# Joining the high and low token parts in one 512-column product of the gate and up matmuls of a two-layer macaron trunk

## The chip, the cores and the metric

The kernel runs on one core of one Trainium2 chip. The metric is device time in microseconds (us) of one execution. Before the change three runs gave a median of 1028.43 us (1027.76 to 1029.43). Engines are named as the profile does: PE multiplies matrices (PEld is its loading of weights), DVE and ACT work element by element, POOL is used here for small vectors and memsets, SP issues nearly all DMAs.

## The reference

Two layers on 256 tokens of width 1024, all in float32. Each layer is a feed-forward block, an attention mixer, and a second feed-forward block; each has its own modulation (shift, scale, gate) out of the vector `c`.

```python
def swiglu(h, w_gate, w_up, w_down):
    return (jax.nn.silu(h @ w_gate) * (h @ w_up)) @ w_down

for l in range(2):
    mod = silu(c) @ ada_w[l] + ada_b[l]             # nine rows of 1024
    sh1, sc1, g1, sh2, sc2, g2, sh3, sc3, g3 = split(mod, 9)
    h = rmsnorm(x, norm_pre[l, 0]) * (1 + sc1) + sh1
    x = x + 0.5 * g1 * rmsnorm(swiglu(h, ...[l, 0]), norm_post[l, 0])
    h = rmsnorm(x, norm_pre[l, 1]) * (1 + sc2) + sh2
    x = x + g2 * rmsnorm(hybrid_mixer(h, ...), norm_post[l, 1])
    h = rmsnorm(x, norm_pre[l, 2]) * (1 + sc3) + sh3
    x = x + 0.5 * g3 * rmsnorm(swiglu(h, ...[l, 1]), norm_post[l, 2])
```

`hybrid_mixer` projects to heads of 64, runs windowed attention on eight heads and block attention on the other eight, and projects back. The hidden width of a feed-forward block is 2816.

## The kernel before

**Products in three parts.** PE works here on the type float32r, which keeps less than float32. Each operand is therefore split: `hi` is the operand rounded to float32r, `lo` is the rest. A product is the sum of three: high by high, high by low, low by high. For weights, `unit` (from L427) loads 1 MB by DMA into a `raw` buffer (three of them); in four or eight pieces ACT writes `hi` (L437) and DVE writes `lo` = raw - hi (L438). For the tokens, `to_T` (from L586) transposes the normed rows on PE, ACT writes the high part (L594) and DVE the low part (L595). They lie in two tiles, `hTh` and `hTl`, each `[128, half, k-tile, 128 tokens]`, with two halves of 128 tokens and eight k-tiles of the width 1024.

**A feed-forward block** (`ffn`, from L664) has two ways to multiply. The first 512 hidden columns go by token half (`rows_of`): tokens stand still in PE, 512 weight columns move. The other 2304 columns go in nine blocks `j` of 256. There the weights stand still and the 256 tokens move, so the result comes out transposed, ready for the down product. For each `j`, gate and up each have a weight unit (`u_both`); for each of its two groups `t` of 128 hidden columns and each of the eight k-tiles, `mm3t` (L480 to L486) issues three products of 256 columns:

```python
nc.tensor.matmul(ps_, wh, hh, start=start, stop=False)   # L484
nc.tensor.matmul(ps_, wh, hl, start=False, stop=False)   # L485
nc.tensor.matmul(ps_, wl, hh, start=False, stop=stop)    # L486
```

The result of both `t` fills one PSUM bank, one for gate and one for up. `swiglu` then applies Silu on ACT (L640, PSUM to SBUF), multiplies with up on DVE (L641, one operand in PSUM), and `split` makes the high and low part of the result (L634 on ACT, L635 on DVE). `down` takes a unit of `w_down` and issues products of 512 columns with `mm3` (L476 to L478) into four banks of accumulators that are kept over the block. PSUM has eight banks: four accumulators, and two buffers under each of two tags for everything else.

**The background.** While the products run, the modulation rows of later steps are computed: `ada_part` loads 512 KB of `ada_w` (L509), DVE sums it (L501), and `over_partitions` (L516 to L519) splits the sum and reduces it over the partitions on PE. A table (`SEC`) says how much of it each step takes.

**The mixer** takes its columns through `mm3t` too (`cols_of`), and its keys through `keys_of`, which clears a tile `kz` with two memsets on POOL (L740, L741) before the keys are copied in. POOL also works out the inverse norms (`rstd_of`, L572 and L574).

**The order.** `keep_order` (from L77) takes the whole program of some 8,000 instructions, gives each a length with `cost` (from L50), plays it through forward (each engine takes the ready instruction of best priority) and backward (how late may each start), four rounds, keeps the shortest, and fixes that order on every engine. An instruction waits in that order even if a later one of its engine is ready. Which instructions depend on each other is found from the ranges of addresses that they touch; a strided access counts as one range from its first to its last element.

Of the kernel before, what the change touches and what calls it, by code (L numbers as in the profile page):

```python
# [11 lines left out]
F32R = mybir.dt.float32r  # L12
# [3 lines left out]
P = 128  # L16
# [34 lines left out]
def cost(ins, eng, slots):  # L51

    kind = type(ins).__name__
    free = math.prod(c for _, c in list(ins.outs[0].ap)[1:])
    if kind == "InstDMACopy":
        return 4 * free * ins.outs[0].ap[0][1] / 360
    if kind == "InstMatmult":
        if ins.is_transpose:
            return 109
        if "float32r" in str(ins.ins[0].dtype):  # L60
            return max(free, 256) / 2.4 + 2.5
        whole = max(4 * free / 2.4 + 4, 160)
        return whole / 4 if ins.outs[0].ap[0][1] == 32 else whole
    src = getattr(ins.ins[0], "bass_ap", None) if ins.ins else None
    psum = src is not None and slots.get(src.tensor.name, "  ")[2] == "PSUM"
    more = [math.prod(c for _, c in list(x.ap)[1:]) for x in ins.ins[1:] if hasattr(x, "ap")]
    if eng == "Activation":
        return (52 if psum else 94) + free / 1.2 + 93 * (len(more) + len(ins.outs) - 1)
    if eng == "DVE":
        if free <= 8:  # L70
            return 75
        single = kind in ("InstTensorScalarPtr", "InstTensorCopy") and max(more, default=1) == 1 and not psum
        return 69 + free / (1.92 if single else 0.96) + 60 * more.count(1)
    return 264 if kind == "InstTensorScalarPtr" else 464


def keep_order(tc, nc, slots, shifts):  # L77
# [20 lines left out]
    for k, ins in enumerate(L):  # L98
        touch = []
        for w, lst in ((False, ins.ins), (True, ins.outs)):  # L100
            for x in lst:
                b = getattr(x, "bass_ap", None)
                if b is None or type(b.tensor).__name__ != "Tile":
                    continue
                name, row = b.tensor.name, math.prod(list(b.tensor.shape)[1:])
                ap, space = list(x.ap), slots[name][2]
                lo = 0 if space == "PSUM" else b.offset if space == "DRAM" else b.offset % row
                hi = 1 << 30
                if space != "PSUM":
                    hi = lo + 1 + sum(abs(s) * (c - 1) for s, c in (ap if space == "DRAM" else ap[1:]))  # L110
                touch.append((w, name, lo, hi))
        for w, name, lo, hi in touch:
# [183 lines left out]
def trunk(ctx, tc, x, c, rel_bias, ada_w, ada_b, norm_pre, norm_post, w_gate, w_up,  # L296
# [176 lines left out]
    def mm3(ps_, hh, hl, wt, wk, sl, start, stop):  # L473
# [4 lines left out]
        nc.tensor.matmul(ps_, hl, wh, start=False, stop=stop)  # L478

    def mm3t(ps_, kt, wt, sl, start, stop):  # L480

        wh, wl = wt[0][:, kt, sl], wt[1][:, kt, sl]
        hh, hl = hT[0][:, :, kt, :], hT[1][:, :, kt, :]
# [92 lines left out]

    hT = [ctile([P, 2, KT, P], f"hT{n}", F32R) for n in "hl"]

# [7 lines left out]
    def to_T(h, k0, nk, src, turned=False):  # L586
# [3 lines left out]
        for t in range(nk):  # L590
            nc.tensor.transpose(p_[:, t * P:(t + 1) * P], src[:, t * P:(t + 1) * P], ident)
        hi, lo = (hT[n][:, h, k0:k0 + nk, :] for n in range(2))
        v = back(p_[:, :nk * P]) if turned else p_[:, :nk * P].rearrange("p (a b) -> p a b", b=P)
# [50 lines left out]
    def rows_of(h, pair, get):  # L644

        for p_, g in zip(pair, get):
            for q in range(2):
                w = g(q)
                for k in range(4):
                    kt = q * 4 + k  # L650
                    mm3(p_, hT[0][:, h, kt, :], hT[1][:, h, kt, :], w, k, slice(0, 512), kt == 0, kt == 7)

# [7 lines left out]
    def ffn(l, i, first):  # L660
# [21 lines left out]
        for j in range(9):  # L682
            cur[0] = j % 2
            if first and j == SETUP:
                with shift(START_SMALL):
                    setup_table(*small)
            pair = (wps(), wps())
            for p_, (tag, ws) in zip(pair, (("g", w_gate), ("u", w_up))):
                w = u_both(l, f, ws, tag, j)
                for t in range(2):  # L690
                    for k in range(KT):
                        mm3t(p_[:, t * 256:(t + 1) * 256], k, w, slice(t * P, (t + 1) * P), k == 0, k == KT - 1)
            act = split(swiglu(*pair), 512)
            for h in range(2):
# [55 lines left out]
    def mixer(h, l):  # L750
# [10 lines left out]
        for k in range(8):  # L761
            mm3(p_[:, :256], hT[0][:, h, k, :], hT[1][:, h, k, :], w, k, slice(0, 256), k == 0, k == 7)
        b_ = brow(512, 256)
# [99 lines left out]
        for u in range(4):  # L863
            w = u_out(l, u)
            for n in range(2):
                for k in range(2):
                    kt = u * 2 + k
                    mm3(accs[n], hT[0][:, h, kt, :], hT[1][:, h, kt, :], w, k, slice(n * 512, (n + 1) * 512),
                        kt == 0, kt == 7)
# [82 lines left out]
    for q in range(4):  # L952
# [12 lines left out]
        for h in range(2):  # L965
# [82 lines left out]
```

## Time and profile before

| | |
|---|---|
| median of three runs | 1028.43 us (1027.76 to 1029.43) |
| the profiled execution | 1027.23 us, its span 1025.5 us |
| PE busy | 1005.2 us, 98% of the span |
| PEld busy (beside PE) | 893.9 us, 87% |
| DVE busy | 800.5 us, 78% |
| ACT busy | 553.5 us, 54% |
| POOL busy | 42.0 us, 4% |
| DMA | 261.95 MB, 255 GB/s over the span |

The span is the profiled execution from its first to its last instruction. A busy share is a mean over stages of different kinds: six steps follow each other (block, mixer, block, twice), the first mixer at about 225 to 345 us, the second at about 715 to 845 us.

### The profile page before, as it was taken

The numbers are of one execution on the slowest core, as the hardware profiler recorded it, in microseconds if no ns is written. First come the engines' busy times: TensorE is split into PE (matmuls) and PEld (weight loads), VectorE is DVE, ScalarE is ACT, GpSimd is POOL, SyncE is SP. The second block draws the span as 40 slices with busy tenths as digits, with TensorE's granted clock in tenths as the row PEclk, the third lists the DMA queues.
The fourth block names the chain that finished last, engine by engine and source line by source line (L and its number), as shares of the span: only waits on it lengthen the run. The fifth ranks groups of instructions, "written<-read, shape, count | busy, mean of one in ns | idle before, by whom it ended". The sixth has DMA issues, their size and how long they took to land. (4 is left out here: it accounts for less than half of the span.)

```text
span 1025.5 us, 17316 instructions
## 1 busy us (share of the span) xinstructions
PE 1005.2 (98%) x6514; PEld 893.9 (87%) x6514; DVE 800.5 (78%) x1493; ACT 553.5 (54%) x1250; POOL 42.0 (4%) x80
## 2 busy tenths in 40 slices
PE   7999999999999999999999999999999999999997
PEld 3699998978887899999979999998798779999996
DVE  4799888978887898798889888886879788555542
ACT  2456443665677665555465445444477766544431
POOL 1000000020002000000010000000100110000000
PEclk9999999999999999999999999999999999999999
DMA  9999998958994588898839887886589638555511
GB/s 328 365 361 325 313 284 295 343 175 279 311 306 168 207 291 295 285 316 311 290 122 308 298 290 284 303 288 226 168 301 323 209 127 272 193 181 189 184 64 41
DMA packets 171855, 261.95 MB, mean 255 GB/s; under 512 B 6396, under 2 KB 107484, under 8 KB 171772
## 3 DMA queue, kind: packets, MB, share of 16 engines
q1 hardware_dynamic: 171616, 260.78, 75.3%
q8 instruction: 51, 0.84, 0.3%
q14 instruction: 32, 0.26, 0.1%
q10 hardware_dynamic: 156, 0.07, 0.0%
HBM read 259.76 MB, written 1.07 MB: 254 GB/s over the span
## 5 line engine op out<-in xcount | busy, mean ns | idle before, releaser
L438 DVE TENSOR_TENSOR lo_a<-raw_a,hi_a 128x512 fp32r<-128x512 f32 (+1 forms) x540 | 294.1, 593 | 43.9 <-issue 23.4
L437 ACT ACTIVATE hi_a<-raw_a 128x512 fp32r<-128x512 f32 (+1 forms) x540 | 259.9, 547 | 123.3 <-PE w_a L485 25.7
L484 PE MATMUL w_a<-hTh,hi_a 128*128 128x256 f32 x768 | 218.9, 285 | 0.6 <-ACT kz_a L733 0.6
L485 PE MATMUL w_a<-hTl,hi_a 128*128 128x256 f32 x768 | 217.8, 284 | 0.0
L486 PE MATMUL w_a<-hTh,lo_a 128*128 128x256 f32 x768 | 217.3, 283 | 0.0
L484 PEld LDWEIGHTS w_a<-hTh,hi_a 128*128 128x128 f32 x768 | 147.1, 192 | 2.2 <-ACT kz_a L733 0.8
L485 PEld LDWEIGHTS w_a<-hTl,hi_a 128*128 128x128 f32 x768 | 147.1, 192 | 1.2 <-issue 0.3
L486 PEld LDWEIGHTS w_a<-hTh,lo_a 128*128 128x128 f32 x768 | 147.0, 191 | 0.4
L485 PE MATMUL w_b<-hTl,hi_b 128*128 128x256 f32 x512 | 144.8, 283 | 0.0
L484 PE MATMUL w_b<-hTh,hi_b 128*128 128x256 f32 x512 | 144.8, 283 | 0.0
L486 PE MATMUL w_b<-hTh,lo_b 128*128 128x256 f32 x512 | 144.7, 283 | 0.0
L437 ACT ACTIVATE hi_b<-raw_b 128x512 fp32r<-128x512 f32 (+1 forms) x224 | 105.1, 544 | 71.3 <-DMA raw_b<-in_ffn_w_up_dram 16.5
L438 DVE TENSOR_TENSOR lo_b<-raw_b,hi_b 128x512 fp32r<-128x512 f32 (+1 forms) x224 | 119.9, 588 | 22.9 <-issue 17.1
L484 PEld LDWEIGHTS w_b<-hTh,hi_b 128*128 128x128 f32 x512 | 98.1, 192 | 1.0
L485 PEld LDWEIGHTS w_b<-hTl,hi_b 128*128 128x128 f32 x512 | 98.1, 192 | 0.9
L486 PEld LDWEIGHTS w_b<-hTh,lo_b 128*128 128x128 f32 x512 | 98.1, 192 | 0.2
L501 DVE SCALAR_TENSOR_TENSOR acc_a<-araw_a,ccol,acc_a 128x512 f32<-128x512 f32 x110 | 82.2, 747 | 12.5 <-DMA araw_a<-in_ada_w_dram 11.0
L477 PE MATMUL a_b<-lo_a,str_a 128*128 128x512 f32 x156 | 60.8, 392 | 0.0
L476 PE MATMUL a_b<-hi_a,str_a 128*128 128x512 f32 x156 | 60.3, 392 | 0.0
L478 PE MATMUL a_b<-hi_a,str_a 128*128 128x512 f32 x156 | 60.2, 390 | 0.0
L501 DVE SCALAR_TENSOR_TENSOR acc_b<-araw_b,ccol,acc_b 128x512 f32<-128x512 f32 x46 | 34.5, 749 | 6.4 <-DMA araw_b<-in_ada_w_dram 5.5
L478 PE MATMUL w_b<-hi_a,hTl 128*128 128x512 f32 (+1 forms) x96 | 36.5, 380 | 0.0
(245 smaller groups left out, 1723.8 us busy)
## 6 DMA issues: line engine op xcount, KB each, us to landing
araw_a<-in_ada_w_dram SPq DMA_DIRECT2D x84, 512.0 KB
raw_a<-in_ffn_w_down_dram SPq DMA_DIRECT2D x30, 1024.0 KB
raw_a<-in_ffn_w_gate_dram SPq DMA_DIRECT2D x26, 1024.0 KB
raw_a<-in_ffn_w_up_dram SPq DMA_DIRECT2D x26, 1024.0 KB
araw_b<-in_ada_w_dram SPq DMA_DIRECT2D x44, 512.0 KB
raw_a<-in_mix_w_in_dram SPq DMA_DIRECT2D x18, 1024.0 KB
raw_b<-in_ffn_w_gate_dram SPq DMA_DIRECT2D x16, 1024.0 KB
raw_b<-in_ffn_w_up_dram SPq DMA_DIRECT2D x16, 1024.0 KB
```

The costliest lines, as they stand in the source:

```text
L437: nc.scalar.activation(hi[:, sl], raw[:, sl], AF.Copy)
L438: nc.vector.tensor_sub(lo[:, sl], raw[:, sl], hi[:, sl].bitcast(F32))
L476: nc.tensor.matmul(ps_, hh, wh, start=start, stop=False)
L477: nc.tensor.matmul(ps_, hh, wl, start=False, stop=False)
L478: nc.tensor.matmul(ps_, hl, wh, start=False, stop=stop)
L484: nc.tensor.matmul(ps_, wh, hh, start=start, stop=False)
L485: nc.tensor.matmul(ps_, wh, hl, start=False, stop=False)
L486: nc.tensor.matmul(ps_, wl, hh, start=False, stop=stop)
L501: nc.vector.scalar_tensor_tensor(acc[:, :n], raw[:, t, :], ccol[:, k:k + 1], b if t == 0 else acc[:, :n], op0=ALU.mult, op1=ALU.add)
```

## The change

There are four parts.

1. The two token tiles become one, `hTa`, `[128, k-tile, high/low, half, 128]`, so that for one k-tile the 256 high and the 256 low columns lie side by side. A new `mm2t` moves all 512 past `wh` in one product, and the 256 high ones past `wl` in a second, which lands on the first 256 columns of the same bank. It takes the place of `mm3t` in the nine `j` of each block alone; the mixer's `cols_of` keeps `mm3t`.
2. Each of the four results of a `j` (gate and up, two `t`) has now a bank of its own, with high-by-low in its second half. ACT copies that half to SBUF, DVE adds the first half to it. Silu and the product with up then work on SBUF, in place.
3. `cost` and the ranges of `keep_order` change: other lengths for DMAs, products and POOL instructions, and a strided access counts as up to 16 separate ranges. The order of all engines is found anew. The tables of numbers stay.
4. `keys_of` clears `kz` in eight pieces where it used two.

```diff
@@ cost
-        return 4 * free * ins.outs[0].ap[0][1] / 360
+        run = 1
+        for step, n in reversed(list(ins.ins[0].ap)):
+            if step != run and n > 1:
+                break
+            run *= n
+        return 4 * free * ins.outs[0].ap[0][1] / (348 if run <= 256 else 388 if run <= 512 else 415)
...
-            return max(free, 256) / 2.4 + 2.5
-        whole = max(4 * free / 2.4 + 4, 160)
+            return free / 2.4 + 13.5
+        whole = max(4 * free / 2.4 + 8, 222)
...
-    return 264 if kind == "InstTensorScalarPtr" else 464
+    return 300 if kind == "InstTensorScalarPtr" else 570 if free == 1 else 170 + 0.76 * free
@@ keep_order
+                dims = [(s, c) for s, c in (ap if space == "DRAM" else ap[1:]) if c > 1]
+                starts = [lo]
+                while len(dims) > 1 and dims[0][0] > 0 and len(starts) * dims[0][1] <= 16:
+                    s, c = dims.pop(0)
+                    starts = [v + s * n for v in starts for n in range(c)]
+                low, size = sum(min(0, s * (c - 1)) for s, c in dims), sum(abs(s) * (c - 1) for s, c in dims)
+                touch += [(w, name, v + low, v + low + size + 1) for v in starts]
@@ trunk
+    def mm2t(ps_, k, wt, sl):
+        for kt in range(k):
+            wh, wl = wt[0][:, kt, sl], wt[1][:, kt, sl]
+            both = lambda **f: nc.tensor.matmul(ps_, wh, hTa[:, kt], **f)
+            if kt < k - 1:
+                both(start=kt == 0, stop=False)
+            nc.tensor.matmul(ps_[:, :256], wl, hT[0][:, kt], start=False, stop=False)
+            if kt == k - 1:
+                both(start=kt == 0, stop=True)
...
-    hT = [ctile([P, 2, KT, P], f"hT{n}", F32R) for n in "hl"]
+    hTa = ctile([P, KT, 2, 2, P], "hT", F32R)
+    hT = [hTa[:, :, n] for n in range(2)]
...
-            pair = (wps(), wps())
-            for p_, (tag, ws) in zip(pair, (("g", w_gate), ("u", w_up))):
+            gu = []
+            for b, (tag, ws) in enumerate((("g", w_gate), ("u", w_up))):
                 w = u_both(l, f, ws, tag, j)
+                gu.append(st())
                 for t in range(2):
-                    for k in range(KT):
-                        mm3t(p_[:, t * 256:(t + 1) * 256], k, w, slice(t * P, (t + 1) * P), k == 0, k == KT - 1)
-            act = split(swiglu(*pair), 512)
+                    p_ = wps(b)
+                    mm2t(p_, KT, w, slice(t * P, (t + 1) * P))
+                    dst = gu[b][:, t * 256:(t + 1) * 256]
+                    nc.scalar.activation(dst, p_[:, 256:], AF.Copy)
+                    nc.vector.tensor_add(dst, p_[:, :256], dst)
+            nc.scalar.activation(gu[0], gu[0], AF.Silu)
+            nc.vector.tensor_mul(gu[0], gu[0], gu[1])
+            act = split(gu[0], 512)
...
-            nc.gpsimd.memset(kv["k"][HD:, :, 0, :], 0.0)
-            nc.gpsimd.memset(kv["k"][:HD, :, 1, :], 0.0)
+            for i in range(4):
+                nc.gpsimd.memset(kv["k"][HD:, i, 0, :], 0.0)
+                nc.gpsimd.memset(kv["k"][:HD, i, 1, :], 0.0)
```

**How the orders differ.** PE, in the first block, where the products of one `j` run; before:

```order
L484 MATMUL w_a_1297<-hTh,hi_a_1301 128x256
L485 MATMUL w_a_1297<-hTl,hi_a_1301 128x256
L486 MATMUL w_a_1297<-hTh,lo_a_1302 128x256
L484 MATMUL w_a_1298<-hTh,hi_a_1381 128x256
L485 MATMUL w_a_1298<-hTl,hi_a_1381 128x256
L476 MATMUL a_b_533<-hi_a_1453,str_a_1040 128x512
```

and in the changed kernel:

```order
L496 MATMUL w_a_897<-hT,hi_a_859 128x512
L499 MATMUL w_a_897<-hT,lo_a_860 128x256 x2
L496 MATMUL w_a_897<-hT,hi_a_859 128x512
L496 MATMUL w_a_933<-hT,hi_a_918 128x512
L499 MATMUL w_a_933<-hT,lo_a_919 128x256
```

Three products of a k-tile have become two, and the 512-column one closes a bank. PE has 1,152 products fewer.

DVE, in the first block, from the first `j` on (`lo` is the low part of a weight unit, `acc` the background sum, `st` a result of gate or up); before:

```order
L438 TENSOR_TENSOR lo_a99_670<-raw_a97_667,hi_a98_669 128x512 x4
L438 TENSOR_TENSOR lo_b104_708<-raw_b102_705,hi_b103_707 128x512
L501 SCALAR_TENSOR_TENSOR acc_b105_717<-araw_b112_791,ccol_112,acc_b105_717 128x512 x2
L438 TENSOR_TENSOR lo_b104_708<-raw_b102_705,hi_b103_707 128x512 x3
L438 TENSOR_TENSOR lo_b110_778<-raw_b108_775,hi_b109_777 128x512
```

and in the changed kernel:

```order
L524 SCALAR_TENSOR_TENSOR acc_b105_692<-araw_b115_757,ccol_112,acc_b105_692 128x512 x2
L721 TENSOR_TENSOR st_a88_548<-w_a89_549,st_a88_548 128x256
L721 TENSOR_TENSOR st_a88_548<-w_a90_568,st_a88_548 128x256
L449 TENSOR_TENSOR lo_a101_647<-raw_a99_644,hi_a100_646 128x512 x2
L721 TENSOR_TENSOR st_a94_599<-w_a95_600,st_a94_599 128x256
L449 TENSOR_TENSOR lo_a101_647<-raw_a99_644,hi_a100_646 128x512
L449 TENSOR_TENSOR lo_b104_683<-raw_b102_680,hi_b103_682 128x512
L721 TENSOR_TENSOR st_a94_599<-w_a96_619,st_a94_599 128x256
```

The additions (L721) stand between the low parts of the next weights (now L449), and the first two of them behind background sums (now L524).

POOL, at the first mixer; before:

```order
L740 MEMSET kz_a_2752 64x4x256
L741 MEMSET kz_a_2752 64x4x256
L572 TENSOR_SCALAR rstd_b_2378<-ss_b_2375 128x1
L574 TENSOR_TENSOR rstd_b_2379<-rstd_b_2378,mhalf 128x1
L572 TENSOR_SCALAR rstd_b_2391<-ss_b_2388 128x1
```

and in the changed kernel:

```order
L772 MEMSET kz_a_2553 64x256
L773 MEMSET kz_a_2553 64x256
L772 MEMSET kz_a_2553 64x256
L595 TENSOR_SCALAR rstd_b_2179<-ss_b_2176 128x1
L773 MEMSET kz_a_2553 64x256
L597 TENSOR_TENSOR rstd_b_2180<-rstd_b_2179,mhalf 128x1
L772 MEMSET kz_a_2553 64x256
```

Three pieces and not the whole tile stand ahead of the second half's inverse norm, one inside it, and the other four behind it.

## Rows read from the trace of the kernel before

**Rows 1.** The page: the span, and busy time of each engine.
```profile
span 1025.5 us, 17316 instructions
...
PE 1005.2 (98%) x6514; PEld 893.9 (87%) x6514; DVE 800.5 (78%) x1493; ACT 553.5 (54%) x1250; POOL 42.0 (4%) x80
```

**Rows 2.** Windows by stage; columns in the order of the first fence line.
```profile
core 0: us, PE busy (x) PEld busy (x) DVE busy (x) ACT busy (x) POOL busy (x), PEclk, DMA share, GB/s
25.00:225.00 200.00, 198.65 (x1332) 177.25 (x1331) 171.27 (x275) 103.92 (x198) 2.81 (x6) 1.00 0.93 317
225.00:345.00 120.00, 116.29 (x702) 98.71 (x702) 101.70 (x227) 83.22 (x222) 13.37 (x22) 1.00 0.73 236
345.00:520.00 175.00, 175.00 (x1184) 162.60 (x1183) 152.82 (x346) 97.17 (x275) 1.52 (x3) 1.00 0.86 292
540.00:715.00 175.00, 175.00 (x1184) 162.57 (x1183) 142.82 (x225) 84.48 (x160) 1.27 (x3) 1.00 0.84 292
715.00:845.00 130.00, 127.10 (x751) 106.77 (x750) 108.53 (x225) 87.08 (x215) 14.75 (x24) 1.00 0.66 220
850.00:1000.00 150.00, 150.00 (x1072) 141.94 (x1071) 84.74 (x135) 69.39 (x127) 0.00 (x0) 1.00 0.53 177
```

**Rows 3.** PE's waits: engine, line, waited for: us in total, times, longest.
```profile
PE w_a L719 <- DVE st_a L765: 3.3, 2, 1.8
```

**Rows 4.** PE's timeline around 120 us: start, us, engine, line, operation.
```profile
119.86 0.39 PE L476 MATMUL a_b<-hi_b,str_b 128*128 128x512 f32 x1
...
122.59 0.39 PE L518 MATMUL w_a<-ast_a,onesr 128*128 128x512 f32 x1
122.82 0.28 PE L484 MATMUL w_a<-hTh,hi_a 128*128 128x256 f32 x1
...
124.97 0.39 PE L519 MATMUL w_a<-ast_a,onesr 128*128 128x512 f32 x1
125.20 0.28 PE L484 MATMUL w_a<-hTh,hi_a 128*128 128x256 f32 x1
```

**Rows 5.** POOL's timeline at the first mixer; idle time in brackets.
```profile
224.81 0.95 POOL L740 MEMSET kz_a<- 64x1024 f32 x1 [3.50 <-PE a_b L478]
225.81 0.95 POOL L741 MEMSET kz_a<- 64x1024 f32 x1
226.86 0.30 POOL L572 TENSOR_SCALAR rstd_b<-ss_b 128x1 f32<-128x1 f32 x1
```

**Rows 6.** Groups by shape: busy us, mean ns, idle before and its releaser.
```profile
L710 POOL MEMSET kzw<- 64x256 f32 x1 | 0.3, 311 | 0.1
...
L595 DVE TENSOR_TENSOR hTl<-w_a,hTh 128x256 fp32r<-128x256 f32 x4 | 1.7, 421 | 0.6 <-ACT hTh L594 0.6
...
L594 ACT ACTIVATE hTh<-w_a 128x256 fp32r<-128x256 f32 x4 | 1.5, 385 | 8.9 <-PE w_a L591 8.9
...
L640 ACT ACTIVATE st_a<-w_a 128x512 f32<-128x512 f32 x23 | 13.6, 593 | 30.4 <-PE w_a L486 30.1 <-PE w_a L478 0.2
...
L634 ACT ACTIVATE str_a<-st_a 128x512 fp32r<-128x512 f32 x20 | 12.5, 626 | 17.5 <-DVE st_a L641 17.5
...
L641 DVE TENSOR_TENSOR st_a<-st_a,w_a 128x512 f32<-128x512 f32 x23 | 15.7, 684 | 16.4 <-PE w_a L486 15.5 <-PE w_a L478 0.8
...
L610 DVE TENSOR_TENSOR st_a<-x,row_a 128x512 f32<-128x512 f32 x6 | 3.9, 684 | 0.0
```

**Rows 7.** Windows inside the first block, columns as in the windows by stage.
```profile
50.00:110.00 60.00, 60.00 (x425) 56.35 (x424) 55.20 (x88) 34.79 (x65) 0.29 (x1) 1.00 0.98 339
170.00:180.00 10.00, 9.06 (x56) 8.00 (x56) 9.86 (x16) 3.87 (x8) 0.00 (x0) 1.00 0.73 241
```

**Rows 8.** ACT's waits from 160 to 200 us, columns as for PE's waits.
```profile
ACT hi_a L437 <- DMA raw_a<-in_ffn_w_down_dram: 7.2, 3, 6.5
...
ACT hi_b L437 <- DMA raw_b<-in_ffn_w_gate_dram: 4.0, 1, 4.0
```

More of the change, by code (lines that the diff above doesn't have):

```diff
@@ L106, in keep_order @@
                 ap, space = list(x.ap), slots[name][2]
[L107 to L111, printed above, removed]
+                if space == "PSUM":
+                    touch.append((w, name, 0, 1 << 30))
+                    continue
+                lo = b.offset if space == "DRAM" else b.offset % row
+                dims = [(s, c) for s, c in (ap if space == "DRAM" else ap[1:]) if c > 1]
[5 more added lines that the diff above has]
+                touch += [(w, name, v + low, v + low + size + 1) for v in starts]
         for w, name, lo, hi in touch:
@@ L478, in mm3 @@
         nc.tensor.matmul(ps_, hl, wh, start=False, stop=stop)
+    def mm2t(ps_, k, wt, sl):
[7 more added lines that the diff above has]
+                both(start=kt == 0, stop=True)
     def mm3t(ps_, kt, wt, sl, start, stop):
         wh, wl = wt[0][:, kt, sl], wt[1][:, kt, sl]
-        hh, hl = hT[0][:, :, kt, :], hT[1][:, :, kt, :]
+        hh, hl = hT[0][:, kt], hT[1][:, kt]
         nc.tensor.matmul(ps_, wh, hh, start=start, stop=False)
@@ L591, in to_T @@
             nc.tensor.transpose(p_[:, t * P:(t + 1) * P], src[:, t * P:(t + 1) * P], ident)
-        hi, lo = (hT[n][:, h, k0:k0 + nk, :] for n in range(2))
+        hi, lo = (hT[n][:, k0:k0 + nk, h, :] for n in range(2))
         v = back(p_[:, :nk * P]) if turned else p_[:, :nk * P].rearrange("p (a b) -> p a b", b=P)
@@ L650, in rows_of @@
                     kt = q * 4 + k
-                    mm3(p_, hT[0][:, h, kt, :], hT[1][:, h, kt, :], w, k, slice(0, 512), kt == 0, kt == 7)
+                    mm3(p_, hT[0][:, kt, h, :], hT[1][:, kt, h, :], w, k, slice(0, 512), kt == 0, kt == 7)
     def hidden_solo(pair):
@@ L761, in mixer @@
         for k in range(8):
-            mm3(p_[:, :256], hT[0][:, h, k, :], hT[1][:, h, k, :], w, k, slice(0, 256), k == 0, k == 7)
+            mm3(p_[:, :256], hT[0][:, k, h, :], hT[1][:, k, h, :], w, k, slice(0, 256), k == 0, k == 7)
         b_ = brow(512, 256)
@@ L867, in mixer @@
                     kt = u * 2 + k
-                    mm3(accs[n], hT[0][:, h, kt, :], hT[1][:, h, kt, :], w, k, slice(n * 512, (n + 1) * 512),
+                    mm3(accs[n], hT[0][:, kt, h, :], hT[1][:, kt, h, :], w, k, slice(n * 512, (n + 1) * 512),
                         kt == 0, kt == 7)
@@ L979, in trunk @@
                         kt = q * 2 + k
-                        mm3(first[h][n], hT[0][:, h, kt, :], hT[1][:, h, kt, :], w, n * 2 + k, slice(0, 512),
+                        mm3(first[h][n], hT[0][:, kt, h, :], hT[1][:, kt, h, :], w, n * 2 + k, slice(0, 512),
                             kt == 0, kt == 7)
```

## The prediction

> **What bounds the kernel now.** I read the page first: PE is busy 1005.2 of 1025.5 us and nothing else is above 87% [rows 1]. A busy share is a mean, so the windows by stage come next. In the second block (345 to 520 us), the third (540 to 715) and the fourth (850 to 1000) PE is busy for the whole stretch, with its clock granted at 1.00, the upper of its two levels (2.4 GHz) [rows 2]. Time taken off PE's products there is time off the end, as long as whatever feeds PE keeps up. The first block (25 to 225 us) is different. PE lacks 1.4 us, DVE is busy for 171.27 of 200 us and the DMA engines for 0.93 of their time [rows 2]. From 50 to 110 us DVE is busy for 55.20 of 60 us, and from 170 to 180 us PE stands still for 0.94 us [rows 7]; around then ACT waits 7.2 us for a `down` weight and 4.0 us for a gate weight [rows 8]. The first block is at three limits at once. In the mixers PE lacks 3.7 us (225 to 345) and 2.9 us (715 to 845) [rows 2]; the greatest single wait there is PE L719 on DVE L765, 3.3 us in two times, one for each mixer [rows 3].
>
> **Fewer products.** The change turns three 256-column products per k-tile into one of 512 and one of 256, for 4 blocks x 9 `j` x 2 matrices x 2 groups x 8 k-tiles = 1152 k-tiles. What a product costs is the step from its start to the next one's, not its listed duration, because durations overlap. From 119.86 to 122.82 us there are 13 products of 512 columns: 2.96 / 13 = 0.2277 us each. From 122.82 to 124.97 there are 18 of 256: 2.15 / 18 = 0.1194 each [rows 4]. Two of 256 take 0.2388, one of 512 takes 0.2277, so a joined pair saves 11.1 ns, and 1152 of them 12.8 us, 3.2 in each block. The columns moved are the same; only the fixed part of one product goes. The lower end is the one place where a 512 is followed by a 256, as it will be everywhere: 124.97 to 125.20, 0.23 us [rows 4], a saving of 8.8 ns or 10.1 us. The upper end is the reading error: starts are given to 0.01 us, so that each step is known to 0.8 ns (512) and 0.6 ns (256, twice), at most 13.1 ns or 15.1 us. I take 11.1 because it rests on 31 products.
>
> One rule speaks against this. The Trainium skill, "TensorE: Matmul & The Clock Gate", section "Back-to-back issue gap", gives an isolated warm gap of N / 2.4 + 2.5 ns, by which a joined pair saves 2.5 ns and the change 2.9 us (an estimate from that page). The trace disagrees: 256 columns take 119.4 ns here, where that gap is 109.2. A fixed part that is smaller than the rows say is kept as a rival.
>
> **More evacuation.** Per block 4 x 9 = 36 results get an ACT copy and a DVE addition, each 128 x 256 out of PSUM. The nearest rows are L594 on ACT, 0.385 us, and L595 on DVE, 0.421 us, same shape and source [rows 6]. That is 13.9 us of ACT and 15.2 us of DVE in each block. Silu moves from PSUM to SBUF, 0.593 (L640) to about 0.626 (L634), nine times, 0.3 us; the product with up is 0.684 with one operand in PSUM (L641) and 0.684 with both in SBUF (L610), no change [rows 6].
>
> What hides this? ACT has room in every block: 103.92 of 200 us in the fullest [rows 2]. DVE would hold 152.82 + 15.2 = 168.0 of 175 - 3.2 = 171.8 us in the second block, 158.0 of 171.8 in the third, 99.9 of 146.8 in the fourth [rows 2]. In those three it fits, with least room in the second, so I cost it at nothing there. The buffer is covered too: a PSUM bank of gate is asked for again after one gate and two up products of 8 k-tiles, 8 x (0.2277 + 0.1194) = 2.8 us each, 8.3 us in all, while copy and addition take 0.8. If the additions come late by more than that, PE stands.
>
> **The first block.** Spread over 200 us, 36 additions put 11 into the stretch from 50 to 110 us: 55.20 + 11 x 0.421 = 59.8 us of DVE work, where PE, 11 x 8 x 11.1 ns = 1.0 us faster, leaves 59.0. From 160 to 190 us the loads are late already [rows 8], and a faster PE meets them sooner. The new order also puts some background loads and sums earlier in this block, ahead of additions, as the order of DVE shows. The bounds: it keeps its whole 3.2 us, or it loses as much again. I take the middle: no gain in the first block, 3.2 of the 12.8 lost. That leaves 9.6.
>
> **The memsets.** At the first mixer two memsets of 0.95 us on POOL hold up the second half's inverse norm: it starts at 226.86, 2.05 us after the first memset began [rows 5]. The order now puts three pieces ahead of it and one inside it. A piece has the shape of L710, 0.311 us [rows 6]; with the gap between memsets (1.00 - 0.95) it is 0.36. Four are 1.44 in place of 2.05: the norm is ready 0.6 us earlier. DVE's normed rows and then its L765 wait for that norm, and PE's L719 for L765. Two mixers give 1.2 us. The bounds are nothing (if another input of L765 comes last) and 3.3, the whole wait [rows 3]. The other four pieces stand behind the norm and are needed only once the keys' product is done.
>
> **The new order.** Lengths and ranges in `keep_order` cost nothing on the chip; they only move instructions. What that is worth no row shows. I put it at zero, and its ends are among the rivals.
>
> **The sum.** 12.8 - 3.2 + 1.2 = 10.8 us. The profiled execution took 1027.23 us, so 1016.4. The median of the three runs, 1028.43, lies 1.2 above that execution, and so I forecast **1017.6 us**. By the page's rule alone the first term would be 2.9 and not 12.8. The ends: 15.1 kept whole and 3.3 in the mixers give 1010.0; 10.1 x 3/4 = 7.6, less 3.2 for the first block, gives 1024.0.
>
> **The rivals.**
>
> - *DVE binds the second block as well.* 168.0 of 171.8 us leaves 2% for waits and clumps [rows 2]. For it: the work comes in clumps, as 50 to 110 us shows [rows 7]. Against it: part of DVE's 152.82 us is overlap of one instruction with the next, and PE there waits for nothing now. It loses that block's 3.2 us and 2 more in the first: 1022.8.
> - *The order gets better through truer lengths.* The mixers' idle time is 3.7 + 2.9 = 6.6 us [rows 2], 1.2 of which I have counted; the other 5.4 would give 1012.2, and with the first block's 3.2 us too 1009.0. Against it: chains of short steps across engines cause that idle time, and they have the same steps as before.
> - *The columns alone set the step.* Then 512 columns that alternate with 256 take what two products of 256 take, 0.2388 us, none of the 12.8 us comes, and the memsets' 1.2 is all: 1027.2. Against it: the steps of 0.2277 and 0.23 [rows 4]. The Trainium skill's gap, "TensorE: Matmul & The Clock Gate", "Back-to-back issue gap", comes near this; three quarters of its 2.9 us would make it 1025.0.
> - *Slower: late additions hold the PSUM banks.* In the first two blocks DVE is fullest. There the additions stand in a fixed order behind background sums and low parts of weights. If one of those waits for its load, the addition waits too, the bank is not free, and PE stands. With 72 results in two blocks and one addition's length each, 72 x 0.421 = 30.3 us is lost against 10.8 gained: 1047.9. It decides from 10.8 / 72 = 0.15 us per result. Against it: the cover of 8.3 us per bank, and PE in the second block waits for nothing now [rows 2].
>
> **The numbers.** Forecast 0.70; DVE binds 0.13; better order 0.09; columns alone 0.03; slower 0.05. The forecast's own range is 1014.5 to 1020.5, half of a block's gain to either side and the median's own spread. The range of 1010 to 1024 takes in the bounds of the costs, the better order in part and DVE's rival; outside lie the best of the better order, the columns alone and the slower case. A measurement of this kernel can tell about 0.2% from no change, 2.1 us: faster is below 1026.3, which all cases but the last two reach, one of them with little room: 0.91 faster, 0.04 the same, 0.05 slower.
>
> **What would show it.** In the changed trace a run of 512 and 256 in turn should step by 0.2277 + 0.1194 = 0.347 us; 0.358, three times 0.1194, would say that the columns alone count. PE should be at its work without a break in the last three blocks, and L721 should not appear among what PE waits for by more than 1 us. DVE should show 36 additions per block at about 0.42 us, ACT 36 copies at 0.39. In the first block some us of PE idle time should appear that were not there, ended by low parts or loads; if there is none, that block kept its 3.2 us. At the mixers PE's wait for L765 should be 0.6 us shorter each. A step of over 0.355 us, PE waits on the additions, or idle time in the second block would make the prediction wrong.

## The result, and the profile after

The changed kernel is slower: a median of 1041.76 us (1039.98 to 1044.97, 4 runs) beside 1028.1 us for the kernel before (1026.71 to 1029.43, 4 runs). The ratio is 1.0146, with a 95% interval of 1.0123 to 1.0169 (the two medians alone give 1.0133). The forecast was 1017.6 us, with a range of 1010.0 to 1024.0. The profiled execution took 1041.14 us.

The page of the changed kernel, its span and busy times, beside [rows 1]:

```profile
span 1039.3 us, 15242 instructions
...
PE 1003.1 (97%) x5362; PEld 832.6 (80%) x5362; DVE 848.8 (82%) x1637; ACT 598.1 (58%) x1394; POOL 43.7 (4%) x92
```

PE has 1,152 products fewer and is busy for only 2.1 us less; outside its busy time it now has 36.2 us and not 20.3. The busy time of DVE went up by 48 us and that of ACT by 45, where the forecast's four blocks at 15.2 and 13.9 us make 61 and 56. The new work has the forecast's size all the same: the lengths of all instructions, added up one by one, rose by 59.5 us on DVE and 55.1 on ACT, while busy time counts an overlap of two instructions once. In the groups of the changed kernel by shape (columns as in [rows 6]) an addition takes 0.419 us and a copy 0.376:

```profile
L721 DVE TENSOR_TENSOR st_a<-w_a,st_a 128x256 f32<-128x256 f32 x80 | 33.2, 419 | 16.4 <-ACT st_a L720 16.2
L720 ACT ACTIVATE st_a<-w_a 128x256 f32<-128x256 f32 x80 | 29.4, 376 | 46.0 <-PE w_a L496 45.7
```

**Where the time went.** Behind each step but the last, PE transposes the normed rows of the second token half. The first of these transposes after each step marks its end. PE's timeline of the kernel before (start, us, engine, line, operation, idle time in brackets):

```profile
232.51 0.66 PE L591 MATMUL w_b<-ident,st_b 128*128 128x128 f32 x4
...
342.10 0.66 PE L591 MATMUL w_b<-ident,st_b 128*128 128x128 f32 x4 [0.46 <-DVE st_b L613]
...
534.09 0.66 PE L591 MATMUL w_b<-ident,st_b 128*128 128x128 f32 x4 [0.31 <-DVE st_b L613]
...
728.38 0.66 PE L591 MATMUL w_b<-ident,st_b 128*128 128x128 f32 x4 [0.21 <-DVE st_b L613]
...
836.64 1.32 PE L591 MATMUL w_b<-ident,st_b 128*128 128x128 f32 x8 [0.39 <-DVE st_b L613]
```

and of the changed kernel:

```profile
239.67 0.66 PE L616 MATMUL w_b<-ident,st_b 128*128 128x128 f32 x4 [0.27 <-DVE st_b L638]
...
354.16 0.66 PE L616 MATMUL w_b<-ident,st_b 128*128 128x128 f32 x4
...
547.68 0.66 PE L616 MATMUL w_b<-ident,st_b 128*128 128x128 f32 x4 [0.32 <-DVE st_b L638]
...
742.75 0.66 PE L616 MATMUL w_b<-ident,st_b 128*128 128x128 f32 x4 [0.27 <-DVE st_b L638]
...
853.44 0.66 PE L616 MATMUL w_b<-ident,st_b 128*128 128x128 f32 x4 [0.48 <-DVE st_b L638]
```

Differences of neighbours, with the spans at the end, give the length of each step in us:

| | block 1 | mixer 1 | block 2 | block 3 | mixer 2 | block 4 | span |
|---|---|---|---|---|---|---|---|
| before | 232.5 | 109.6 | 192.0 | 194.3 | 108.3 | 188.9 | 1025.5 |
| changed | 239.7 | 114.5 | 193.5 | 195.1 | 110.7 | 185.9 | 1039.3 |
| difference | +7.2 | +4.9 | +1.5 | +0.8 | +2.4 | -3.0 | +13.8 |

The fourth block, which holds only 4 of the 256 background sums (L524), gained 3.0 us, near the 3.2 of the forecast; the joined products' own share of that is 2.2 to 2.4 us by the steps below. All others lost, the first block and the mixers most, and the mixers have no joined product at all.

**The joined products do save.** PE's timeline of the changed kernel in the fourth block, through the two results of one weight unit (the middle rows repeat):

```profile
904.68 0.40 PE L496 MATMUL w_a<-hT,hi_a 128*128 128x512 f32 x1
904.91 0.28 PE L499 MATMUL w_a<-hT,lo_a 128*128 128x256 f32 x1
905.03 0.40 PE L496 MATMUL w_a<-hT,hi_a 128*128 128x512 f32 x1
905.26 0.28 PE L499 MATMUL w_a<-hT,lo_a 128*128 128x256 f32 x1
...
910.08 0.40 PE L496 MATMUL w_a<-hT,hi_a 128*128 128x512 f32 x1
910.32 0.40 PE L487 MATMUL a_b<-hi_a,str_a 128*128 128x512 f32 x1
```

From 904.68 to 910.32 there are 16 pairs: 0.3525 us each. The longest stretches without any other product run, in the changed kernel, over 61 pairs:

```profile
472.80 0.39 PE L496 MATMUL w_b<-hT,hi_b 128*128 128x512 f32 x1
...
494.24 0.39 PE L541 MATMUL w_b<-ast_b,onesr 128*128 128x512 f32 x1
```

and in the one before over 184 products:

```profile
459.27 0.28 PE L484 MATMUL w_b<-hTh,hi_b 128*128 128x256 f32 x1
...
481.34 0.39 PE L518 MATMUL w_b<-ast_b,onesr 128*128 128x512 f32 x1
```

That is 0.3514 us for a pair and 0.3599 for three: 8.4 ns saved per k-tile, 9.7 us in all, where 11.1 ns and 12.8 us were forecast. A stretch of 32 k-tiles in the fourth block (932.97 to 944.24 us, before 917.77 to 929.28) gives 7.5 ns, so the saving is known to about 1 ns.

**The new waits.** PE's waits in the changed kernel, columns as in [rows 3]:

```profile
PE w_a L541 <- DVE st_a L721: 5.8, 2, 3.6
...
PE w_b L541 <- DVE st_b L721: 1.8, 1, 1.8
PE w_a L750 <- DVE st_a L797: 1.8, 2, 1.0
PE w_b L496 <- DVE row_b L555: 1.7, 2, 1.1
```

The first two are new: the background product L541 needs a PSUM bank, and both banks of its tag hold results of gate or up that an addition has yet to read. DVE's timeline before the longest of them:

```profile
642.08 0.42 DVE L721 TENSOR_TENSOR st_a<-w_a,st_a 128x256 f32<-128x256 f32 x1
644.17 0.75 DVE L524 SCALAR_TENSOR_TENSOR acc_a<-araw_b,ccol,acc_a 128x512 f32<-128x512 f32 x1 [1.68 <-DMA araw_b<-in_ada_w_dram]
644.84 0.69 DVE L449 TENSOR_TENSOR lo_b<-raw_b,hi_b 128x512 fp32r<-128x512 f32 x1
645.44 0.42 DVE L721 TENSOR_TENSOR st_a<-w_a,st_a 128x256 f32<-128x256 f32 x1
645.78 1.88 DVE L449 TENSOR_TENSOR lo_b<-raw_b,hi_b 128x512 fp32r<-128x512 f32 x3
647.58 0.74 DVE L524 SCALAR_TENSOR_TENSOR acc_a<-araw_b,ccol,acc_a 128x512 f32<-128x512 f32 x1
648.24 0.41 DVE L721 TENSOR_TENSOR st_a<-w_a,st_a 128x256 f32<-128x256 f32 x1
```

and PE's at that place:

```profile
648.71 0.50 PE L541 MATMUL w_a<-ast_a,onesr 128*128 128x512 f32 x1 [3.58 <-DVE st_a L721]
```

A background sum waits 1.68 us for its load. Two additions stand behind it, and in front of the second four more instructions. When that addition is done at 648.6, PE, idle for 3.58 us, goes on. This is the mechanism of the slower rival in the forecast, at another price: three waits of 7.6 us in all, and on one background product each. Two of them are in the first block; they say nothing yet about the rest of its loss, or about the mixers.

**The memsets.** POOL's timeline at the first mixer, beside [rows 5]:

```profile
232.02 0.31 POOL L772 MEMSET kz_a<- 64x256 f32 x1 [3.26 <-PE a_b L489]
232.36 0.30 POOL L773 MEMSET kz_a<- 64x256 f32 x1
232.72 0.31 POOL L772 MEMSET kz_a<- 64x256 f32 x1
233.13 0.30 POOL L595 TENSOR_SCALAR rstd_b<-ss_b 128x1 f32<-128x1 f32 x1
```

The norm starts 1.11 us after the first piece and not 2.05, and PE's wait for the mixer's first rows (L719 before, L750 now) fell from 3.3 to 1.8 us in two. No mixer got shorter, though.

### The profile page after: what moved, and what is told of

Read it like the earlier page. It is cut to its first block, busy times and chain, and to the rows that moved or that the text cites. A ratio compares the mean times of both kernels' runs of the same rounds, so it can differ in the third digit from the quotient of the medians.

```text
span 1039.3 us, 15242 instructions
## 1 busy us (share of the span) xinstructions
PE 1003.1 (97%) x5362; PEld 832.6 (80%) x5362; DVE 848.8 (82%) x1637; ACT 598.1 (58%) x1394; POOL 43.7 (4%) x92
## 5 line engine op out<-in xcount | busy, mean ns | idle before, releaser
L449 DVE TENSOR_TENSOR lo_a<-raw_a,hi_a 128x512 fp32r<-128x512 f32 (+1 forms) x540 | 295.5, 592 | 23.2 <-PE w_a L499 8.4
L496 PE MATMUL w_a<-hT,hi_a 128*128 128x512 f32 x640 | 224.1, 397 | 0.2 <-DVE st_b L721 0.2
L496 PE MATMUL w_b<-hT,hi_b 128*128 128x512 f32 x512 | 180.3, 397 | 1.7 <-DVE row_b L555 1.7
L499 PE MATMUL w_a<-hT,lo_a 128*128 128x256 f32 x640 | 167.0, 282 | 0.5 <-DVE lo_a L449 0.3
L496 PEld LDWEIGHTS w_a<-hT,hi_a 128*128 128x128 f32 x640 | 116.7, 188 | 22.9 <-PE w_a L496 0.5
L499 PE MATMUL w_b<-hT,lo_b 128*128 128x256 f32 x512 | 133.2, 281 | 0.2 <-DVE lo_b L449 0.2
L449 DVE TENSOR_TENSOR lo_b<-raw_b,hi_b 128x512 fp32r<-128x512 f32 (+1 forms) x224 | 122.5, 588 | 13.0 <-PE w_a L499 5.5
L499 PEld LDWEIGHTS w_a<-hT,lo_a 128*128 128x128 f32 x640 | 120.5, 189 | 8.5 <-DVE lo_a L449 1.4
L496 PEld LDWEIGHTS w_b<-hT,hi_b 128*128 128x128 f32 x512 | 93.7, 188 | 20.7 <-DVE row_b L555 2.5
L499 PEld LDWEIGHTS w_b<-hT,lo_b 128*128 128x128 f32 x512 | 96.6, 189 | 6.4 <-DVE lo_b L449 0.5
L524 DVE SCALAR_TENSOR_TENSOR acc_a<-araw_a,ccol,acc_a 128x512 f32<-128x512 f32 x110 | 82.1, 747 | 15.4 <-DMA araw_a<-in_ada_w_dram 14.1
L721 DVE TENSOR_TENSOR st_a<-w_a,st_a 128x256 f32<-128x256 f32 x80 | 33.2, 419 | 16.4 <-ACT st_a L720 16.2
L507 PE MATMUL w_a<-hT,hi_a 128*128 128x256 f32 x128 | 37.0, 292 | 0.9 <-ACT kz_a L764 0.6
L487 PE MATMUL w_a<-hi_a,hT 128*128 128x512 f32 (+1 forms) x96 | 36.5, 380 | 0.2 <-DVE hT L620 0.2
## 6 DMA issues: line engine op xcount, KB each, us to landing
raw_a<-in_ffn_w_down_dram SPq DMA_DIRECT2D x30, 1024.0 KB
raw_a<-in_ffn_w_gate_dram SPq DMA_DIRECT2D x26, 1024.0 KB
raw_a<-in_ffn_w_up_dram SPq DMA_DIRECT2D x26, 1024.0 KB
raw_a<-in_mix_w_in_dram SPq DMA_DIRECT2D x18, 1024.0 KB
raw_b<-in_ffn_w_gate_dram SPq DMA_DIRECT2D x16, 1024.0 KB
raw_b<-in_ffn_w_up_dram SPq DMA_DIRECT2D x16, 1024.0 KB
```

What stands on the lines that cost most here:

```text
L449: nc.vector.tensor_sub(lo[:, sl], raw[:, sl], hi[:, sl].bitcast(F32))
L487: nc.tensor.matmul(ps_, hh, wh, start=start, stop=False)
L496: both = lambda **f: nc.tensor.matmul(ps_, wh, hTa[:, kt], **f)
L499: nc.tensor.matmul(ps_[:, :256], wl, hT[0][:, kt], start=False, stop=False)
L524: nc.vector.scalar_tensor_tensor(acc[:, :n], raw[:, t, :], ccol[:, k:k + 1], b if t == 0 else acc[:, :n], op0=ALU.mult, op1=ALU.add)
L721: nc.vector.tensor_add(dst, p_[:, :256], dst)
```

## The experiments

Three theories at first. **Bank:** late additions hold PSUM banks. **Order:** the new lengths and ranges in `keep_order` put steps in worse places. **Load:** the additions fill DVE. Step lengths below are read as in the table above. Each ratio is to runs of the kernel before on the same chip, with its 95% interval.

**Only the order (e1).** The kernel before with the new `cost` and the new ranges:

```diff
-        return 4 * free * ins.outs[0].ap[0][1] / 360
+        return 4 * free * ins.outs[0].ap[0][1] / (348 if run <= 256 else 388 if run <= 512 else 415)
...
-            return max(free, 256) / 2.4 + 2.5
-        whole = max(4 * free / 2.4 + 4, 160)
+            return free / 2.4 + 13.5
+        whole = max(4 * free / 2.4 + 8, 222)
...
-                touch.append((w, name, lo, hi))
+                touch += [(w, name, v + low, v + low + size + 1) for v in starts]
```

> The kernel before (1028.1 us), with only the new lengths in cost and the new ranges in keep_order; products, banks and memsets as before. Bank theory (PE's background product L541 and the products behind it wait for a bank that a late addition on DVE still holds; in the changed trace such stalls are 2.0 us at 116, 2.4 at 180, 3.7 at 649): nothing of that kind exists without the additions, so 1026 to 1030 us. Order theory (the new lengths misplace steps in the mixers, which took 4.6 and 1.8 us longer, and loads in the first block, 7.5 us longer): 1034 to 1042. Load theory (the additions fill DVE, so that low parts of weights come late): 1026 to 1030.

Measured: 1053.22 us, ratio 1.0248 (1.0224 to 1.0271). The order alone, with the products as before, costs more than the whole change, and more than any of the theories had put it at. Block 1 takes 251.6 us there, and its two longest stalls are in it. PE's timeline of that kernel at one of them:

```profile
141.87 0.23 PE L412 MATMUL w_b<-ident,small_a 16*128 16x16 f32 x1
142.03 0.81 PE L417 MATMUL w_b<-small_a,small_a 32*16 32x384 f32 x2
150.82 0.58 PE L495 MATMUL w_b<-hTh,hi_b 128*128 128x256 f32 x1 [7.98 <-ACT bq L415]
151.20 0.42 PE L496 MATMUL w_b<-hTl,hi_b 128*128 128x256 f32 x1
151.42 0.41 PE L497 MATMUL w_b<-hTh,lo_b 128*128 128x256 f32 x1
151.63 0.41 PE L495 MATMUL w_b<-hTh,hi_b 128*128 128x256 f32 x1
```

and ACT's timeline, which PE waited for:

```profile
147.03 2.19 ACT L448 ACTIVATE hi_a<-raw_a 128x512 fp32r<-128x512 f32 x4 [4.19 <-DMA raw_a<-in_ffn_w_gate_dram]
149.12 0.61 ACT L645 ACTIVATE str_a<-st_a 128x512 fp32r<-128x512 f32 x1
150.00 0.63 ACT L527 ACTIVATE ast_b<-acc_b 128x512 fp32r<-128x512 f32 x1 [0.27 <-DVE acc_b L512]
150.54 0.16 ACT L414 ACTIVATE bq<-w_b 128x8 f32<-128x8 f32 x1
150.60 0.17 ACT L415 ACTIVATE bq<-w_b 128x8 f32<-128x8 f32 x1
```

PE's small product is done at 142; its evacuation `bq`, two copies of 0.16 and 0.17 us, stands in the fixed order behind the high part of a weight unit that waits 4.19 us for its load, and behind two more conversions. PE waits 7.98 us for the bank. Behind that the products step by 0.21 us in place of 0.12: PE has fallen to the lower of its two clock levels (1.2 GHz) after standing idle; the granted clock is 0.50 from 145 to 154 us, and its mean from 110 to 170 us is 0.91, where it was 1.00 before. So one order pays twice.

**The old lengths under the joined products (e2).**

```diff
-        return 4 * free * ins.outs[0].ap[0][1] / (348 if run <= 256 else 388 if run <= 512 else 415)
+        return 4 * free * ins.outs[0].ap[0][1] / 360
...
-            return free / 2.4 + 13.5
-        whole = max(4 * free / 2.4 + 8, 222)
+            return max(free, 256) / 2.4 + 2.5
+        whole = max(4 * free / 2.4 + 4, 160)
...
-    return 300 if kind == "InstTensorScalarPtr" else 570 if free == 1 else 170 + 0.76 * free
+    return 264 if kind == "InstTensorScalarPtr" else 464
```

> The changed kernel (1041.8 us) with the old cost; products, banks, ranges and memsets as changed. Order theory: the mixers go back to 119.9 and 119.5 us and the first block gives back some of its 7.5: 1028 to 1035. Bank theory and load theory: the order shifts the stalls about but does not remove them, 1038 to 1045.

Measured: 1025.59 us, ratio 0.9993 (0.9974 to 1.0011). From 1.0146 to 0.9993 the lengths in `cost` account for 1.5%, some 16 us. The mixers are back at 109.6 and 108.6 us; the longest wait of a background product on an addition shrinks to 0.7 us, without any change to the additions or banks. PE's waits there:

```profile
PE w_b L611 <- DVE st_b L870: 2.2, 2, 1.3
PE w_a L745 <- DVE st_a L792: 1.8, 2, 1.2
...
PE w_a L536 <- DVE st_a L716: 0.7, 1, 0.7
```

**Other banks (e3)** and **no additions (e4)**, both with the new lengths:

```diff
-                    p_ = wps(b)
+                    p_ = wps()
```

> The changed kernel, but all four results of a j take banks of the tag of that j (even or odd, as before the change) and not gate one tag and up the other. The background product, which takes the other tag, then meets banks that were left one j ago. Bank theory: the stalls of 2 to 4 us in front of L541 go, 1030 to 1035 us. Order theory: no better, 1039 to 1044. Load theory: no better, 1039 to 1044, or worse, since each bank must now be free again after one product in place of three.

```diff
-                    nc.scalar.activation(dst, p_[:, 256:], AF.Copy)
-                    nc.vector.tensor_add(dst, p_[:, :256], dst)
+                    nc.scalar.activation(dst, p_[:, :256], AF.Copy)
```

> The changed kernel without the 144 additions: ACT copies the first 256 columns and the second 256, the high weights by the low tokens, are left out of the result. PE's products, the lengths and the memsets stay. Load theory and bank theory: DVE loses 60 us of work and no bank waits for it, so the products' 10 us show in full outside the mixers, 1020 to 1028 us. Order theory: the mixers and the first block stay slow, 1034 to 1040.

Measured: e3 1045.88 us, 1.0177 (1.0152 to 1.0202), no better. e4 1036.64 us, 1.0104 (1.0072 to 1.0136), 4 to 5 us better than the change, with intervals that overlap. Even without a single addition it stays slower than before, with block 1 at 238.3 and the mixers at 115.2 and 111.9 us, so the load of the additions doesn't explain most of the loss. e4 does not rule out the bank theory: its order was found anew, and in it a late copy on ACT holds a bank as a late addition did. Out of PE's waits and ACT's timeline of e4:

```profile
PE w_b L496 <- ACT st_b L720: 5.9, 1, 5.9
...
146.47 2.19 ACT L448 ACTIVATE hi_a<-raw_a 128x512 fp32r<-128x512 f32 x4 [4.11 <-DMA raw_a<-in_ffn_w_gate_dram]
148.56 0.61 ACT L539 ACTIVATE ast_b<-acc_b 128x512 fp32r<-128x512 f32 x1
149.09 0.36 ACT L720 ACTIVATE st_b<-w_b 128x256 f32<-128x256 f32 x1
```

The copy stands behind the high part of a unit that waits 4.11 us for its load, and PE waits 5.9 us for the copy. So a held bank is one of the ways in which an order costs time, and not a rival to the order. That the order decides how much it costs is shown by e2, where the same additions and banks cost 0.7 us at most at one place.

**Which length?** The DMA rates put back alone (e5), the DMA rates new alone (e6), another DMA rate with old lengths (e7), the products' lengths new alone (e8, and each of its two halves, e9 and e10). Each edit is one of the lines of the diff above; e7 has 340 in place of 360.

> The changed kernel (1041.8 us) with one thing put back: cost gives every DMA the old 360 bytes per ns again, in place of 348, 388 or 415. DMA theory (with the rates too high the order puts instructions that wait for a load ahead of others that PE waits for; ACT and DVE together wait for loads 71.0 us in the first block of the changed kernel, 43.5 with all old lengths): 1023 to 1030 us, first block under 237. Product theory (the longer products of cost misplace the rest): 1037 to 1044. Chance theory (any other set of lengths throws the order by some 10 us either way): anywhere in 1025 to 1045.

> The reverse: the changed kernel with the old cost but for the new DMA rates. DMA theory: 1035 to 1045 us, with waits for loads of ACT and DVE of 60 us or more in the first block. Product theory: as with all old lengths, 1024 to 1028. Chance theory: anywhere in 1025 to 1045.

> The changed kernel with the old cost (1025.6 us with that), and the DMA rate lower still, 340 for all. DMA theory: what looks late in the plan is put later in the order, so that less waits in front: 1018 to 1026 us, waits for loads in the first block under 43.5. Chance theory: anywhere in 1020 to 1040; product theory: 1024 to 1028.

> The changed kernel with the old cost but for the new lengths of products (the joined product 227 ns in place of 216, one of 256 columns 120 in place of 109). DMA theory: 1022 to 1028 us, about as with all old lengths. Product theory: 1035 to 1044. Chance theory: anywhere in 1025 to 1045.

> The changed kernel with the old cost (1025.6 us), but for the new length of float32r products alone (256 columns 120 ns in place of 109). Split of the 10 us that the new lengths of products cost. Theory of one bad length, this one: 1033 to 1038 us, the first mixer at 114 or more (109.6 with the old lengths, 117.1 with both new ones). If it is the other: 1023 to 1028. Tuned-table theory (the tables of pace and lead fit the old lengths, and any other lengths give a worse order, however true): 1028 to 1036, losses in several steps.

> The same for the new length of plain float32 products alone (64 columns 222 ns in place of 160; the trace has two rows of 111 for one such product, so the new one is the true one). If this length is the bad one: 1033 to 1038 us, the first mixer at 114 or more, where these products stand. If not: 1023 to 1028. Tuned-table theory: 1028 to 1036.

| joined products, lengths | us | ratio (95%) | block 1 | mixer 1 | block 2 | block 3 | mixer 2 | block 4 |
|---|---|---|---|---|---|---|---|---|
| all old (e2) | 1025.6 | 0.9993 (0.9974 to 1.0011) | 234.9 | 109.6 | 190.1 | 193.0 | 108.6 | 186.2 |
| old, DMA at 340 (e7) | 1029.0 | 1.0027 (1.0010 to 1.0043) | 236.1 | 110.8 | 190.7 | 195.7 | 108.1 | 185.8 |
| new float32r (e9) | 1029.3 | 1.0016 (0.9991 to 1.0040) | 236.8 | 111.5 | 190.4 | 192.0 | 108.5 | 186.3 |
| new float32 (e10) | 1030.8 | 1.0017 (0.9998 to 1.0036) | 235.1 | 110.5 | 189.5 | 197.1 | 111.5 | 185.8 |
| both products new (e8) | 1035.6 | 1.0081 (1.0054 to 1.0108) | 236.3 | 117.1 | 190.1 | 192.8 | 110.7 | 186.3 |
| new DMA (e6) | 1032.3 | 1.0047 (1.0022 to 1.0073) | 234.1 | 114.1 | 189.3 | 196.5 | 111.7 | 186.0 |
| all new but DMA (e5) | 1033.9 | 1.0076 (1.0046 to 1.0106) | 235.3 | 116.0 | 192.7 | 193.1 | 112.1 | 185.9 |
| all new (the change) | 1041.8 | 1.0146 (1.0123 to 1.0169) | 239.7 | 114.5 | 193.5 | 195.1 | 110.7 | 185.9 |

No single length is the culprit. Beside e2, the DMA rates come to about 0.5%, the products' lengths to 0.9%, all together to 1.5%. A lower DMA rate, where the DMA theory had hoped for a gain, brought none. But e7, e9 and e10 lie inside the spread that four random orders show below (0.9975 to 1.0029), and e6 only just outside: a cost of those lengths by themselves isn't shown. The new POOL lengths had no run of their own; e5 and e8 differ by them alone and agree within their intervals. The loss lies mostly in the mixers and in block 1.

**Is it chance?** If any disturbance costs time, the direction of the lengths says nothing. So every length was multiplied by a random number, first with the old lengths under the joined products (e11, e12, later e17, e18), then in the kernel before (e13, e14), and with the new lengths (e15, e16):

```diff
-    dur = [cost(i, e, slots) for i, e in zip(L, eng)]
+    rnd = np.random.default_rng(1)
+    dur = [cost(i, e, slots) * (1 + 0.02 * (2 * rnd.random() - 1)) for i, e in zip(L, eng)]
```

> The changed kernel with the old cost, each length multiplied by a random number between 0.98 and 1.02 (first seed): no length is truer or less true on the whole. Tuned-table theory, and chance: 1028 to 1040 us, since the order that came out with the old lengths is a lucky or tuned one. Theory that certain lengths are bad: 1023 to 1028, as with the old cost.

> The same with a second seed, and the same expectation: 1028 to 1040 us where the order of the old lengths is a tuned or lucky one, 1023 to 1028 where the order only suffers from certain lengths. The spread between the two seeds is what a change of order without any reason is worth.

> The kernel before (1027.3 us), each length of its cost multiplied by a random number between 0.98 and 1.02 (first seed). Its tables were set with exactly its lengths. Tuned-order theory: it loses some us, 1030 to 1042, and then the joined products, which with jitter took 1030.1 and 1025.7, gain more than the 1.6 us seen beside the order of the old lengths: some 5 to 10. Theory that the order of before is nothing special: 1025 to 1030, and the joined products are worth about nothing but in the last block.

> The same with the second seed and the same expectation: 1030 to 1042 us if the order of before is a tuned one, 1025 to 1030 if it is nothing special.

> The changed kernel (1041.8 us) with its own new lengths, each multiplied by a random number between 0.98 and 1.02 (first seed). Chance theory (the order of the change is one unlucky draw): 1025 to 1038 us, as wide apart as the seeds are. Theory that the new lengths, with these tables, are bad as such: 1036 to 1046, as the change itself.

> The same with the second seed and the same expectation: 1025 to 1038 us by chance, 1036 to 1046 if the new lengths are bad with these tables.

> The changed kernel with the old cost and 2% jitter, third seed: another draw of the order. If joined products are worth some 6 us between orders of equal luck (1030.1 and 1025.7 with, 1034.4 and 1033.2 without), 1024 to 1031 us; if the gap of the first seeds was chance, 1032 to 1036. The second, third and fourth block should take 189 to 191, 192 to 195 and 186 us of its span, where those without joined products took 192, 194.3 and 188.5.

> The same with a fourth seed, and the same expectation: 1024 to 1031 us, or 1032 to 1036 if the gap was chance. A version under 1025 would beat the second seed, the best so far.

| jitter of 2% | us | ratio (95%) | block 1 | mixer 1 | block 2 | block 3 | mixer 2 | block 4 |
|---|---|---|---|---|---|---|---|---|
| before, seed 1 (e13) | 1034.4 | 1.0065 (1.0040 to 1.0090) | 235.3 | 114.0 | 192.0 | 194.4 | 110.3 | 188.7 |
| before, seed 2 (e14) | 1033.2 | 1.0061 (1.0040 to 1.0083) | 232.9 | 113.4 | 192.1 | 194.2 | 112.0 | 188.3 |
| joined, old, seed 1 (e11) | 1030.1 | 1.0025 (1.0003 to 1.0047) | 232.7 | 112.7 | 189.2 | 194.7 | 111.5 | 186.0 |
| joined, old, seed 2 (e12) | 1025.7 | 0.9975 (0.9955 to 0.9995) | 232.3 | 110.3 | 189.2 | 192.7 | 112.0 | 186.0 |
| joined, old, seed 3 (e17) | 1026.6 | 0.9977 (0.9958 to 0.9995) | 233.5 | 108.5 | 189.2 | 192.5 | 112.6 | 185.8 |
| joined, old, seed 4 (e18) | 1031.4 | 1.0029 (1.0010 to 1.0049) | 233.9 | 112.9 | 188.7 | 196.5 | 109.9 | 186.0 |
| joined, new, seed 1 (e15) | 1042.6 | 1.0160 (1.0112 to 1.0208) | 241.0 | 116.6 | 190.5 | 193.2 | 111.0 | 185.9 |
| joined, new, seed 2 (e16) | 1049.6 | 1.0220 (1.0190 to 1.0251) | 240.4 | 118.9 | 190.2 | 194.3 | 121.0 | 185.9 |

Three things follow.

- The order of the kernel before seems to be a good one. Two draws with 2% jitter lose 0.6% each, all of it in block 1 and the mixers: blocks 2, 3 and 4 keep their lengths to 0.6 us. More draws were not taken.
- Without the new lengths the change is a gain between such draws. With jitter on both sides the mean ratio is 1.0002 (four draws) against 1.0063 (two), 0.6% or some 6 us, roughly, since the four alone differ by up to 0.5%. Block 2 gains 3 us and block 4 some 2.5 in every draw, block 3 between 1.8 us gained and 2.2 lost. Beside the order that the kernel before really has, only e12 and e17 are ahead.
- The new lengths are bad with this kernel's tables, and not by one unlucky draw. Three orders with them (the change, e15, e16) have ratios of 1.0146 to 1.0220, five with the old ones (e2 and four draws) 0.9975 to 1.0029. Block 1 takes 239.7 to 241.0 us against 232.3 to 234.9.

e12 and e17 are faster than both kernels, by 0.25% and 0.23% (intervals that just leave out 1). They are e2 with another draw, and nothing in them is better for a reason. e12 also fell below the 1028 to 1040 us that a lucky or tuned order had led me to expect.

**What stays open.** Why truer lengths give worse orders isn't shown. The new lengths of products agree with the steps in [rows 4] (227.7 ns against 227 in `cost`, 119.4 against 120); those of DMAs and POOL were not set against a trace here. A possible reason is that the tables (`SEC`, the leads, `BACKLOG`) were set beside the old lengths and would have to be set anew, but no run set them anew. The new ranges in `keep_order` were never run by themselves.

## Why the prediction was wrong

**The new order: the step that failed.** "Lengths and ranges in `keep_order` cost nothing on the chip; they only move instructions. What that is worth no row shows. I put it at zero". The runs put it at 1.5%, some 16 us slower (e2 against the change), and at 2.5% with the products as before (e1). It had ends among the rivals only on the faster side, "the order gets better through truer lengths". With it at 16 us, the remaining sum, 10.8 us gained, gives about 1034, and with the first term at its measured size 1037; the change measured 1041.8, because the remaining sum did not come either. With the old lengths (e2) it was worth 0.7 us and not 10.8: blocks 2, 3 and 4 gained 1.9, 1.3 and 2.7 us where 3.2 each were forecast, the first block lost 2.4, and the mixers gained nothing. Part of that may be a good order that the kernel before had and another draw loses (e13, e14); two draws can't say how much. The comparison of orders stood there before the forecast, and showed background loads and sums moved ahead of additions; I read it for the places and not as a cost of its own.

**Fewer products.** The term was mis-sized: 7.5 to 8.4 ns for each joined pair and not 11.1, 9.7 us at most and not 12.8. The step of a 512 followed by a 256 (0.23 us) in [rows 4] was the better row, 8.8 ns, and I took the one that rested on more products of the wrong neighbours. The Trainium skill's isolated gap, "TensorE: Matmul & The Clock Gate", section "Back-to-back issue gap", would have left 2.5 ns per pair (an estimate from that page); the 8.4 ns of the trace disagree with it, though less than I said. The rival that the columns alone count fell.

**More evacuation.** Right in size (0.419 and 0.376 us for 0.421 and 0.385), and right that it can be hidden in blocks 2 and 4 under an order that suits it: e2 and the draws take 189 to 190 and 186 us there. Block 3, at 192.5 to 196.5 us, gains in some of these orders and loses in others. The cover of 8.3 us per bank was wrong: I counted the next gate result as the next user, but the background product L541 takes a bank of the same tag in between.

**The slower rival** named the right mechanism for part of the loss, additions behind background sums that wait for a load. In the changed trace it cost three waits of 7.6 us in all and not 30, and it hangs on the order as well: under the old lengths the longest such wait is 0.7 us (e2).

**The first block** was forecast to gain nothing. Under the old lengths it took 234.9 us against 232.5, and 232.3 to 233.9 in the four draws; under the new ones 239.7. So "no gain" was near the mark without the order (0.2 us gained to 2.4 lost), though that its causes were the ones forecast isn't shown, and the order's 5 us came on top.

**The memsets.** The norm came even earlier than worked out (1.11 us after the first piece, not 1.44), and PE's wait for it fell by 1.5 us where 1.2 was forecast. The mixers gained nothing by it: 109.6 and 108.6 us in e2, 109.6 and 108.3 before. In e2 PE waits 1.8 us for the first rows, as in the changed kernel, and now 2.2 us in two, one in each mixer, for the normed rows of a head group (L611 on DVE L870), a wait that the kernel before doesn't have. Whether that took the gain was not tested.

## What to carry to other kernels

Where a fixed order comes out of a search with hand-set tables, a change to the search's inputs is a change to every engine's order. Give it a cost of its own, on both sides, however true the new inputs are, and measure it apart from the change that it came with. Before a gain of under 1% is read into such a kernel, jitter the inputs on both sides: here the draw alone was worth up to 0.6%, as much as the edit.

## What the runs showed that I had not expected

- A 512-column product between products of 256 steps by more than one in a run of its like: the pair takes 0.3514 us where the two steps of [rows 4] add up to 0.3471.
- A single evacuation of 0.2 us (`bq`) that stands behind one waiting load in its engine's order cost PE 7.98 us, and then the clock's lower level on top (steps of 0.21 us in place of 0.12).
- 2% of random jitter on all lengths moved the result by up to 0.5% between four draws (ratios of 0.9975 to 1.0029).
